# A one-core hybrid attention/mLSTM layer: earlier operand tiles for the second token span, weight sums formed on the fly, and mixer results left in SBUF

## The chip, the cores and the metric

The kernel runs on one core of a Trainium2 chip. The metric is device time in microseconds of one launch; lower is better. The engines are TensorE (PE; its weight loads are shown apart as PEld), VectorE (DVE), ScalarE (ACT), GpSimd (POOL) and SyncE (SP, which here issues nearly all DMAs). SBUF is the memory beside the engines, PSUM holds eight banks that matmuls accumulate into, and DRAM is the chip's far memory.

## What is computed

One layer of an encoder for 2048 tokens of width 1024, in float32. Cut to what matters:

```python
xn = rms_norm(x, mix_norm_g)
aq, ak, av, mq, mk, mv, mo, ipre, fpre, ga, gm = split(xn @ w_in)
att = chunk_band_attention(aq, ak, av, rel_bias)         # 8 heads of 64, own chunk of 64 and 8 before it
mq, mk = silu(causal_conv4([mq, mk]))
hm = mlstm_chunkwise(mq, mk, mv, ipre + b_i, fpre + b_f) # 4 heads of 128, a recurrence over the tokens
m = sigmoid(mo) * headwise_rms_norm(hm)
y = sigmoid(ga) * (att @ w_att_proj) + sigmoid(gm) * (m @ w_mlstm_proj)
x = x + y @ w_out
x = x + square(relu(rms_norm(x) @ w_up)) @ w_down        # hidden width 4096
out = rms_norm(x) * final_norm_g
```

## The kernel before, in words

**Arithmetic.** Every float32 operand is split into a rounded part and a remainder, and each product is three matmuls (high by high, high by low, low by high). The large products also use a seven-product form of 2x2 block multiplication, so each 2x2 block of weights and of operands is turned into seven sums and differences. On the operand side these are called m = 0 to 6, with four tiles (k = 0 to 3) for each m. On the weight side a block is a "quad" of four 512 KB tiles a, b, c, d, and its sums are b-a, d-(b-a), d-b and c-(d-(b-a)).

**Tokens.** The 2048 tokens are four blocks of 512 (b = 0 to 3), in two spans (s = 0: blocks 0 and 1; s = 1: blocks 2 and 3). The stages follow each other on TensorE in `dense` (L832):

1. `token_tiles` (L558): values of blocks 0 and 1.
2. Nine quads of input weights for span 0 (`quad`, L601), in the order `IN_FIRST`. Index i counts them.
3. `in_far` (L665): all input products of span 1, in three batches of operands, `BATCHES = ((0, 3, 1), (2, 4), (5, 6))`, over the eleven weight columns of `IN_ORDER`. Index g counts the batches, i the columns. A partial result goes to a DRAM tensor `park` after batches 0 and 1 (`park_u2`, `park_v`) and comes back through `unpark` (L755), which is started when batch 1 or 2 starts; `finish_far` (L772, its addition is L776) adds it to PSUM. Blocks 0 and 1 of the mixers (attention and mLSTM) run beside it, and `project` (L924) multiplies their results by the two projection weights.
4. Span 0: two quads of `w_out`, eight quads of `w_up`, then `down` (L801), seven times over m, with the mixers of blocks 2 and 3 and their two `project` calls beside it.
5. Span 1: the same two, eight and seven, then the final norm.

**What orders the work.** The program is written by a planner (`Flow`, L104). Each piece of work is a generator that asks for tiles of a pool, waits for events, and then yields the name of an engine, a cost in ns and a delay; the planner grants engines by earliest start, then by priority (0 first), and emits the instructions in that order. So each engine, and SP's DMA queue, runs a fixed order of instructions that follows from estimates such as `yield "sp", 900, 2000` (a 256 KB transfer) and `yield "sp", 1750, 2000` (512 KB). On the chip an instruction that waits holds up everything behind it on its engine or queue.

**Pools.** `wraw` (4 tiles of 512 KB, weights as loaded), `wsp` (3 tiles, split weights), `r` (28 tiles, split operands), `ctx` (16 tiles of 256 KB), `tmp` (6 tiles of 256 KB), `bias` (2), `sc` (4), and the eight PSUM banks.

**Weights.** `loader` (L388) follows `weights` (L357). A quad comes in one of three ways:

- `part`, seven loads: three given tiles and four sums that `sum_w` (L420) formed earlier and stored in the DRAM tensor `wsum`. `sum_w` takes four `ctx` tiles twice, for eight loads, eight subtractions (L437) and eight stores of 256 KB.
- `quad` with `kept` true (`quad_w`, L499): four loads of 512 KB into all four `wraw` tiles, four subtractions of 128x1024 (L512), and four stores of the sums to `wsum` for a later use.
- `quad` with `kept` false: the same without the stores. Before the change nothing uses this.

`SUMS` (L59) lists which quad's sums are formed at which place: seven from the start of the kernel through stage 2 (among them both `w_out` quads and the first two `w_up` quads), two in batch 0 of stage 3, one in batch 1, five in the `w_up` quads of span 0. Every weight tile is then split by ACT (L493) and DVE (L495).

**Operands of span 1.** `stats_far` (L1007) reads blocks 2 and 3 of x, sixteen pieces one after the other through one `tmp` tile at a time, and forms each block's scale (POOL, L1027). `rows_far(1)` spreads the scales over the partitions. `take_x1` (L1607) for each k takes five `tmp` tiles at once, loads four pieces of x (L1615), scales them (L1618), forms the seven sums (L1678) and stores them to the DRAM tensor `xu` (L1957). These are started at i = 5 of stage 2. `take_batches` (L784) reads them back into `r` tiles (L2011) and splits them when the last quad of stage 2 frees its 28 `r` tiles.

**Mixer results.** An attention unit (`weigh`, L1201) or an mLSTM head (`rec_head`, L1492) stores its result to the DRAM tensor `mix` (`keep_mix`, L1239). `load_mix` (L914) starts eight threads that each wait for one result, take an `r` tile, load it and split it (`take_u1`, L2009; ACT L1079, DVE L1084), and `project` waits for all eight.

**Down operands.** `take_u` (L1994) takes 8 `r` tiles (16 in span 1) as a ring for the squared `w_up` results that `down` reads back from the DRAM tensor `u`; it is started at the last but one `w_up` quad. For span 0, `reserve` (L797) then takes 8 more for the results of block 2, and `mixers(2)` starts attention and recurrence, which take `r` tiles as well.

Of the kernel before, what the change touches and what calls it, by code (L numbers as in the profile page):

```python
# [30 lines left out]
D = 1024  # L31
# [218 lines left out]
class Layer:  # L250
# [106 lines left out]
    def weights(self):  # L357
# [62 lines left out]
    def sum_w(self, q, after=()):  # L420
# [3 lines left out]
        for h in range(2):  # L424
# [5 lines left out]
            for n, x in ((0, a), (1, c), (3, d), (2, b)):  # L430
                yield "sp", 900, 2000
# [12 lines left out]
    def load_w(self, src, raw, ev):  # L444
        yield "sp", 1750, 2000
# [3 lines left out]
    def split_w(self, i, src, raw, sent=None):  # L449
# [4 lines left out]
        yield "sp", 1750, 2000  # L454
# [6 lines left out]
    def split_first(self, src, raw, sent):  # L461
# [5 lines left out]
        for k, ev in enumerate(evs):  # L467
            yield "sp", 900, 2000
# [30 lines left out]
    def quad_w(self, i, q, kept, raws, evs):  # L499
# [5 lines left out]
        def keep(n, raw):  # L505
            yield "sp", 1750, 2000
# [158 lines left out]
    def in_far(self, A, aev, ring):  # L665
# [7 lines left out]
        for g, batch in enumerate(BATCHES):  # L673
            got = [[[None, None] for _ in range(2)] for _ in IN_ORDER]
            gev = [[E2() for _ in range(2)] for _ in IN_ORDER]
            room = Pool([0] * (4 + 2 * g))
            if g > 0:
                fl.spawn(self.unpark(g, kept, got, gev, room), 1)
            if g == 1:
                self.load_mix(0, ring)  # L680
            for i, name in enumerate(IN_ORDER):
                self.sum_at(g + 1, i)
                if (g, i) in PROJ_IN:
                    b = PROJ_IN[g, i]
                    yield from self.project(b, ring)
                    if b == 0:
                        fl.spawn(self.take_batch(BATCHES[2], A, aev, ring), 1)
                        self.load_mix(1, ring)
# [66 lines left out]
    def unpark(self, g, kept, got, gev, room):  # L755
        for i, name in enumerate(IN_ORDER):
            o = off(name)
            for x in range(g)[::-1]:
                for n in range(2):
# [4 lines left out]
                    yield "sp", 900, 2000  # L764
# [32 lines left out]
    def reserve(self, room, n, after=()):  # L797
        yield "wait", list(after)
        for _ in range(n):
            self.fl.put(room, *(yield "get", self.rpool, 1))  # L800
    def down(self, s, m, ring, A, aev, blocks, room):  # L801
# [4 lines left out]
        for c in range(4):  # L806
            for b in blocks:
                if PROJ[b][1] == c:
                    yield from self.project(b, room)
                    if b == 2:  # L810
                        self.load_mix(3, room)
# [20 lines left out]
    def dense(self):  # L832
# [15 lines left out]
        for i, name in enumerate(IN_FIRST):  # L848
# [8 lines left out]
            if i == 5:  # L857
# [11 lines left out]
        for s in range(NS):  # L869
# [6 lines left out]
            for i in range(N_F):  # L876
# [37 lines left out]
    def load_mix(self, b, room):  # L914
        for x in range(8):
            self.fl.spawn(self.load_mix1(b, x, room), 1)

    def load_mix1(self, b, x, room):
        B = self.blk[b]
        yield "wait", [B["mix_ev"][x]]  # L920
        (r,) = yield "get", room, 1
        B["mix"][x] = r
        yield from self.take_u1(self.mixd.ap()[b, x], r, B["mixed"][x])
# [19 lines left out]
    def load_gates(self, b, gates, go):  # L943
# [4 lines left out]
        for j in range(0, KT, 2):  # L948
            yield "wait", [go[j // 2]] if j > 0 else self.blk[b]["mix_ev"][:7]
            for x in range(2):  # L950
                for n in range(2):
# [3 lines left out]
                    yield "sp", 900, 2000  # L955
# [51 lines left out]
    def stats_far(self):  # L1007

        fl, nc = self.fl, self.nc
        for b in (2, 3):  # L1010
            r, q = self.rin[b], self.rq
            for t in range(NT):
                for g in range(2):
                    (x,) = yield "get", self.temp, 1
                    x5 = x[:, :T]
                    yield "sp", 900, 2000
# [33 lines left out]
    def square_in(self, b, k, x, tot, ev):  # L1050
# [5 lines left out]
        yield "sp", 900, 2000  # L1056
# [33 lines left out]
    def attention(self, b):  # L1090
# [6 lines left out]
        for j in range(4):  # L1097
# [3 lines left out]
            for x, to in zip((b, b - 1), vs):  # L1101
                yield "sp", 900, 2000
# [4 lines left out]
            for i in range(2):  # L1107
                h = 2 * j + i
                k, q = yield "get", self.rpool, 2
                fl.spawn(self.head(b, h, vs, k, q), 1)  # L1110
        fl.set(B["kq_all"])
        yield "wait", B["head_done"]
        fl.put(self.rpool, *pt)
    def head(self, b, h, vs, k, q):
# [3 lines left out]
        for n, x in ((0, b - 1), (1, b)):  # L1118
# [3 lines left out]
            yield "sp", 900, 2000  # L1122
# [3 lines left out]
        yield "sp", 900, 2000  # L1126
# [74 lines left out]
    def weigh(self, b, h, u, pieces, slots, pev, done):  # L1201
# [30 lines left out]
        fl.put(self.banks, bk)  # L1232
        yield "dve", dve_ns(256)
        nc.vector.tensor_add(tmp[own, :256], tmp[own, :256], tmp[own, 256:512])
        cols = slice(u * 256, u * 256 + 256)
# [3 lines left out]
    def keep_mix(self, b, x, dst, src, pool, *items):  # L1239
        fl, B = self.fl, self.blk[b]  # L1240
        yield "sp", 900, 2000
        self.nc.sync.dma_start(dst, src)
        fl.put(pool, *items)
        B["mix_left"][x] -= 1
        if B["mix_left"][x] == 0:
            fl.set(B["mix_ev"][x])

# [53 lines left out]
    def gates(self, b, bk, less=None, more=False):  # L1301
# [5 lines left out]
        if more:  # L1307
            (add,) = yield "get", self.temp, 1
            yield "wait", [self.gate_ev]
            yield "sp", 900, 2000  # L1310
# [157 lines left out]
    def load_rec(self, b, h):  # L1468
# [5 lines left out]
        for to, x in ((k, MH + h), (q, h)):  # L1474
            yield "wait", [self.m_ev[b, x]]
            yield "sp", 900, 2000
# [3 lines left out]
        yield "sp", 900, 2000  # L1480
# [11 lines left out]
    def rec_head(self, b, h, r):  # L1492
# [75 lines left out]
        yield "sp", 900, 2000  # L1568
# [867 lines left out]
```

## Time and profile before

| | |
|---|---|
| device time, 3 runs | median 2812.18 us (2805.07 to 2813.29) |
| profiled execution, its own time | 2812.02 us |
| its span, first to last instruction | 2810.2 us |
| ACT busy | 1538.8 us (55%) |
| POOL busy | 37.6 us (1%) |
| weight loads, PEld busy | 2280.1 us (81%) |
| moved by DMA | 737.50 MB, mean 262 GB/s |
| weight tiles loaded as given, from `wf` | 188 of 512 KB |
| sums loaded from `wsum` | 176 of 512 KB |
| DVE, splits of weights (L495) | 453 x 1220 ns |
| DVE, subtractions of 128x1024 (L512) | 56 x 1219 ns |
| DVE, subtractions of 128x512 in `sum_w` (L437) | 120 x 684 ns |

How to read it: a view by windows gives, for each stretch of the span, the busy time of every engine, the granted clock of TensorE as a mean share of full speed, and the share of time that the sixteen DMA engines moved packets. A matmul is recorded from its start until its result is out, so consecutive matmuls overlap; when TensorE never waits, starts follow each other closely and its busy time equals the stretch. "idle before <- X" is time in which an engine stood still and what ended it.

### The profile page before, as it was taken

Reading aid. Unit: us, or ns where it says so; the run is one execution under the profiler, and the core shown is the slowest. Engines: PE = TensorE matmul, PEld = TensorE weight load, DVE = VectorE, ACT = ScalarE, POOL = GpSimd, SP = SyncE. Lnnn points to the kernel's source line nnn. Section 1 sums busy time; section 2 is a strip of 40 time slices with the busy share of each in tenths; the row PEclk is TensorE's granted clock in tenths of the full one; section 3 lists DMA queues with packets and bytes.
Section 4 is the critical chain, followed back from the end, with each engine's and each line's share of the span. In section 5 each row is a group of like instructions: output and inputs, shape, how many; then the busy total and the mean of one; then the engine's idle time right before and its main releaser. Section 6 shows DMA issues by size and latency. Waiting matters only on the chain.

```text
span 2810.2 us, 38516 instructions
## 1 busy us (share of the span) xinstructions
PE 2752.5 (98%) x12916; PEld 2280.1 (81%) x12916; DVE 2053.5 (73%) x3684; ACT 1538.8 (55%) x2636; POOL 37.6 (1%) x108
## 2 busy tenths in 40 slices
PE   9999997999999999999999999999999999999998
PEld 8778886788888777788888887888888888888887
DVE  7877765887887767885777789778877664457675
ACT  6545454765663433565555676566444665555443
POOL 0000000000000000000000000000000000000000
PEclk9999998999999999999999999999999999999999
DMA  8777689888888899977878887877777475578773
GB/s 283 274 257 258 238 288 301 277 273 272 265 297 290 300 311 321 318 247 266 309 270 292 272 277 239 249 217 244 258 266 245 169 260 206 205 268 271 268 250 128
DMA packets 353402, 737.50 MB, mean 262 GB/s; under 512 B 39524, under 2 KB 66788, under 8 KB 353204
## 3 DMA queue, kind: packets, MB, share of 16 engines
q1 hardware_dynamic: 353060, 735.04, 77.7%
q8 instruction: 101, 1.65, 0.2%
q14 instruction: 97, 0.79, 0.1%
q10 hardware_dynamic: 144, 0.01, 0.0%
HBM read 498.89 MB, written 236.01 MB: 262 GB/s over the span
## 4 chain that ended last, share of the span: by engine, by line
PE 80%; DVE 7%; DMA 6%; issue 3%; ACT 2%; SPq 1%; POOL 0%; POOLq 0%; ACTq 0%; DVEq 0%
PE bank L623 38%; PE bank L554 8%; PE bank L555 8%; PE bank L556 8%; PE bank L654 8%; PE bank L1218 2%; PE bank L1291 2%; DVE wsp L495 2%; PE bank L659 2%; PE bank L1260 2%; DMA ctx<-park 1%; DMA r<-u 1%; DMA r<-mix 1%; ACT wsp L493 1%; DVE sc L1266 1%
## 5 line engine op out<-in xcount | busy, mean ns | idle before, releaser
L623 PE MATMUL bank<-r,wsp 128*128 128x512 f32 x4872 | 1114.5, 390 | 2.7 <-ACT r L1081 1.0
L623 PEld LDWEIGHTS bank<-r,wsp 128*128 128x128 f32 x4872 | 912.8, 188 | 198.3 <-issue 1.9
L493 ACT CAST wsp<-wraw 128x1024 fp32r<-128x1024 f32 x453 | 475.9, 1051 | 525.0 <-PE bank L623 221.2
L495 DVE TENSOR_TENSOR wsp<-wraw,wsp 128x1024 fp32r<-128x1024 f32 x453 | 552.7, 1220 | 287.3 <-ACT wsp L493 275.8
L554 PE MATMUL bank<-r,wsp 128*128 128x512 f32 x1152 | 454.8, 395 | 2.3 <-ACT r L1079 1.7
L555 PE MATMUL bank<-r,wsp 128*128 128x512 f32 x1152 | 449.5, 390 | 0.0
L556 PE MATMUL bank<-r,wsp 128*128 128x512 f32 x1152 | 448.9, 390 | 0.0
L654 PE MATMUL bank<-r,wsp 128*128 128x512 f32 x1512 | 373.3, 395 | 5.3 <-DVE ctx L776 4.6
L654 PEld LDWEIGHTS bank<-r,wsp 128*128 128x128 f32 x1512 | 278.8, 189 | 62.9 <-DVE ctx L776 3.5
L556 PEld LDWEIGHTS bank<-r,wsp 128*128 128x128 f32 x1152 | 216.3, 188 | 45.8
L554 PEld LDWEIGHTS bank<-r,wsp 128*128 128x128 f32 x1152 | 216.4, 188 | 44.4 <-ACT r L1079 2.1
L555 PEld LDWEIGHTS bank<-r,wsp 128*128 128x128 f32 x1152 | 216.6, 188 | 40.6 <-DVE r L1084 0.2
L1079 ACT CAST r<-r 128x512 fp32r<-128x512 f32 x284 | 171.7, 621 | 121.2 <-DMA r<-u 89.9
L1084 DVE TENSOR_TENSOR r<-r 128x512 fp32r<-128x512 f32 x284 | 188.8, 685 | 65.0 <-ACT r L1079 64.2
L1711 DVE TENSOR_TENSOR ctx<-bank,ctx 128x512 f32<-128x512 f32 x150 | 103.1, 688 | 96.5 <-PE bank L623 96.0
L1272 ACT ACTIVATE sc<-sc,scs 128x640 f32<-128x640 f32 (+4 forms) x128 | 97.3, 760 | 65.5 <-DVE scs L1266 64.9
L1703 ACT COPY ctx<-bank 128x512 f32<-128x512 f32 x150 | 87.0, 581 | 56.9 <-PE bank L623 55.9
L2027 ACT ACTIVATE ctx<-ctx 128x512 f32<-128x512 f32 x96 | 60.5, 630 | 84.0 <-DVE ctx L1711 83.9
L1296 DVE TENSOR_TENSOR r<-bank,r 128x512 fp32r<-128x512 f32 (+1 forms) x168 | 95.8, 592 | 11.7 <-ACT r L1294 11.1
L1218 PE MATMUL bank<-r,r 128*128 128x512 f32 x336 | 97.9, 373 | 4.5 <-DVE r L1296 3.1
L1260 PE MATMUL bank<-r,r 128*128 128x320 f32 (+3 forms) x480 | 91.2, 309 | 5.9 <-DMA r<-kfar 2.6
L1294 ACT CAST r<-bank 128x512 fp32r<-128x512 f32 (+1 forms) x168 | 80.5, 517 | 22.6 <-PE bank L1291 20.0
(246 smaller groups left out, 2996.3 us busy)
## 6 DMA issues: line engine op xcount, KB each, us to landing
wraw<-in_wf SPq DMA_DIRECT2D x188, 512.0 KB, 4.5
wraw<-wsum SPq DMA_DIRECT2D x176, 512.0 KB, 4.4
r<-u SPq DMA_DIRECT2D x224, 256.0 KB, 4.5
u<-ctx SPq DMA_DIRECT2D x128, 256.0 KB, 2.3
ctx<-in_wf SPq DMA_DIRECT2D x120, 256.0 KB, 4.3
wsum<-ctx SPq DMA_DIRECT2D x120, 256.0 KB, 3.8
wsum<-wraw SPq DMA_DIRECT2D x56, 512.0 KB, 3.3
u<-tmp SPq DMA_DIRECT2D x96, 256.0 KB, 3.0
```

Source lines behind the costliest of these rows:

```text
L493: nc.scalar.copy(w[:, 0], raw)
L495: nc.vector.tensor_sub(w[:, 1], raw, w[:, 0].bitcast(F32))
L554: mm(ps, lh, rh, start=first, stop=False)
L555: mm(ps, lh, rl, start=False, stop=False)
L556: mm(ps, ll, rh, start=False, stop=last)
L623: mm(ps, wv[:, x, k, n], a[:, y], start=new and k == 0 and x == y == 0, stop=k == 3 and x == 1, skip_group_check=True)
L654: mm(ps, wv[:, x, k, n], a[:, y], start=start and x == y == 0, stop=stop and x == 1, skip_group_check=True)
L1079: self.nc.scalar.copy(dst[:, 0], src)
L1084: self.nc.vector.tensor_sub(dst[:, 1], src, dst[:, 0].bitcast(F32))
L1218: nc.tensor.matmul(bkv[:, :, c0:c0 + w], st, sl[:, :, o:o + w], start=n == 0, stop=n == total - 1)
L1260: nc.tensor.matmul(bks[x][:, :w], q[:, y, i * P:(i + 1) * P], kf[:, f * P + x * w:f * P + x * w + w], start=y == 0, stop=y == 1)
L1711: nc.vector.tensor_add(t[:, o:o + 512], ps, t[:, o:o + 512])
```

## The change

- **Operands early.** `rows_far(1)` and the four `take_x1` start at i = 2 of stage 2 and no longer at i = 5.
- **Weights on the fly.** All `w_out` and `w_up` quads, in both spans, come as `quad` with `kept` false. `SUMS` drops the four quads that were summed ahead for them; the eight `w_down` quads are summed at two places in batch 0 of stage 3 and six in the `w_up` quads of span 0.
- **Mixer results on chip.** `take_mix` takes the eight `r` tiles of a block at once, where `load_mix` was started. A result of block 2, and of any other block once those tiles are there, is split straight into them by ACT and DVE; only other results go through `mix`.
- **Order of tiles at the end of `w_up`, span 0.** `take_u` and `reserve` wait until the first two attention heads of block 2 have their tiles (`begun`), and `take_u` is started one quad later.
- **Park early.** `unpark` for batch 2 starts at the last column of batch 1, with the same room of eight tiles.
- **Planner.** The cost of a 256 KB transfer on SP is 800 instead of 900, of a 512 KB one 1570 instead of 1750, everywhere; the seven operands of a k get priorities by m.

The diff's core (the SP costs, repeated on many lines, are shown once):

```diff
+DIRECT = (2,)
 N_IN = 16
-N_USUM = 2
-SUMS = {(0, n): q for n, q in enumerate((Q_IN[IN_FIRST[0]], Q_VM, Q_VM + 1, N_G, N_G + 1, N_G + N_O, N_G + N_O + 1))}
-SUMS.update({at: N_Q - N_F + n for n, at in enumerate(((1, 2), (1, 7), (2, 2), (4, 0), (4, 1), (4, 2), (4, 3), (4, 4)))})
+SUMS = {(0, n): q for n, q in enumerate((Q_IN[IN_FIRST[0]], Q_VM, Q_VM + 1))}
+SUMS.update({at: N_Q - N_F + n for n, at in enumerate(((1, 4), (1, 8), *((4, i) for i in range(6))))})
...
-            yield from (part(q, m) for q in range(N_G, N_G + N_O) for m in range(7))
-            for q in range(N_G + N_O, N_G + N_O + N_F):
-                if s == 0 and q >= N_G + N_O + N_USUM:
-                    yield "quad", (q, True)
-                else:
-                    yield from (part(q, m) for m in range(7))
+            for q in range(N_G, N_G + N_O + N_F):
+                yield "quad", (q, False)
...
-        yield "sp", 1750, 2000
+        yield "sp", 1570, 2000
...
-            if g == 1:
-                self.load_mix(0, ring)
+            if g == 1:
+                fl.spawn(self.take_mix(0, ring), 1)
             for i, name in enumerate(IN_ORDER):
                 self.sum_at(g + 1, i)
+                if g == 1 and i == len(IN_ORDER) - 1:
+                    ahead = ([[[None, None] for _ in range(2)] for _ in IN_ORDER], [[E2() for _ in range(2)] for _ in IN_ORDER],
+                             Pool([0] * 8))
+                    fl.spawn(self.unpark(2, kept, *ahead), 1)
...
-            if i == 5:
+            if i == 2:
                 ready, read = Event(), [Event() for _ in range(4)]
                 fl.spawn(self.rows_far(1, ready, read), 2)
                 for k in range(4):
                     fl.spawn(self.take_x1(k, ready, read[k]), 2)
...
-                    fl.spawn(self.take_u(s, ring, *D), 0)
+                    if s == 1:
+                        fl.spawn(self.take_u(s, ring, *D), 0)
                 if s == 0 and i == N_F - 1:
-                    fl.spawn(self.reserve(room, 8, self.blk[2]["vp_ev"][:1]), 0)
-                    self.load_mix(2, room)
+                    fl.spawn(self.take_u(s, ring, *D, self.blk[2]["begun"]), 0)
+                    fl.spawn(self.reserve(room, 8, self.blk[2]["begun"]), 0)
+                    fl.spawn(self.take_mix(2, room), 1)
                     self.mixers(2)
...
+        direct = self.direct(b, h // 2)
         yield "dve", dve_ns(256)
         nc.vector.tensor_add(tmp[own, :256], tmp[own, :256], tmp[own, 256:512])
-        cols = slice(u * 256, u * 256 + 256)
+        if direct:
+            yield "wait", [B["mix_got"]]
+            r = B["mix"][h // 2]
+            yield "act", act_ns(256)
+            nc.scalar.copy(r[own, 0, cols], tmp[own, :256])
+            yield "dve", dve_ns(256)
+            nc.vector.tensor_sub(r[own, 1, cols], tmp[own, :256], r[own, 0, cols].bitcast(F32))
+            fl.put(self.temp, tmp)
+            self.mix_done(b, h // 2)
+            fl.set(done)
+            return
...
+    def direct(self, b, x):
+        how, got = self.blk[b]["how"], self.blk[b]["mix_got"]
+        return how.setdefault(x, b in DIRECT or got.at is not None)
...
+    def take_mix(self, b, room):
+        B = self.blk[b]
+        B["mix"] = yield "get", room, 8
+        self.fl.set(B["mix_got"])
...
-        fl.spawn(self.keep_mix(b, 4 + h, self.mixd.ap()[b, 4 + h], kt[:, :512], self.ctx, kt), 1)
+        if self.direct(b, 4 + h):
+            yield "wait", [B["mix_got"]]
+            yield from self.split(kt[:, :512], B["mix"][4 + h])
+            self.mix_done(b, 4 + h)
+            fl.put(self.ctx, kt)
+        else:
+            fl.spawn(self.keep_mix(b, 4 + h, self.mixd.ap()[b, 4 + h], kt[:, :512], self.ctx, kt), 1)
...
-            fl.spawn(give(m, dst), 1)
+            fl.spawn(give(m, dst), 1 + m / 100)
```

More of the change, by code (lines that the diff above doesn't have):

```diff
@@ L673, in in_far @@
         for g, batch in enumerate(BATCHES):
[L674 to L677, printed above, removed]
+            if g < 2:
+                got = [[[None, None] for _ in range(2)] for _ in IN_ORDER]
+                gev = [[E2() for _ in range(2)] for _ in IN_ORDER]
+                room = Pool([0] * (4 + 2 * g))
+            else:
+                got, gev, room = ahead
+            if g == 1:
                 fl.spawn(self.unpark(g, kept, got, gev, room), 1)
             if g == 1:
-                self.load_mix(0, ring)
+                fl.spawn(self.take_mix(0, ring), 1)
             for i, name in enumerate(IN_ORDER):
                 self.sum_at(g + 1, i)
+                if g == 1 and i == len(IN_ORDER) - 1:
+                    ahead = ([[[None, None] for _ in range(2)] for _ in IN_ORDER], [[E2() for _ in range(2)] for _ in IN_ORDER],
+                             Pool([0] * 8))
+                    fl.spawn(self.unpark(2, kept, *ahead), 1)
                 if (g, i) in PROJ_IN:
@@ L687, in in_far @@
                         fl.spawn(self.take_batch(BATCHES[2], A, aev, ring), 1)
-                        self.load_mix(1, ring)
+                        fl.spawn(self.take_mix(1, ring), 1)
                     else:
@@ L795, in take_batch, with reserve @@
                 fl.spawn(self.take_u1(self.xud.ap()[m, k], r, aev[m][k]), 0)
-    def reserve(self, room, n, after=()):
-        yield "wait", list(after)
+    def reserve(self, room, n, after=None):
+        if after is not None:
+            yield "wait", [after]
         for _ in range(n):
@@ L810, in down @@
                     if b == 2:
-                        self.load_mix(3, room)
+                        fl.spawn(self.take_mix(3, room), 1)
                     else:
@@ L912, in mixers @@
             fl.spawn(self.attention(b), 1)
[L914 to L923, printed above, removed]
     def project(self, b, room):
@@ L1110, in attention @@
                 fl.spawn(self.head(b, h, vs, k, q), 1)
+            if j == 0:
+                fl.set(B["begun"])
         fl.set(B["kq_all"])
@@ L1246, in keep_mix, with load_mix @@
             fl.set(B["mix_ev"][x])
+            if self.direct(b, x):
+                fl.set(B["mixed"][x])
+            else:
+                fl.spawn(self.load_mix(b, x), 1)
+    def direct(self, b, x):
+        how, got = self.blk[b]["how"], self.blk[b]["mix_got"]
+        return how.setdefault(x, b in DIRECT or got.at is not None)
+    def load_mix(self, b, x):
+        B = self.blk[b]
+        yield "wait", [B["mix_got"]]
+        yield from self.take_u1(self.mixd.ap()[b, x], B["mix"][x], B["mixed"][x])
+    def take_mix(self, b, room):
+        B = self.blk[b]
+        B["mix"] = yield "get", room, 8
+        self.fl.set(B["mix_got"])
     def scores(self, b, i, k, q, bias, sct, ev):
@@ L1626, in load @@
             yield "wait", [kept[b][j]]
-            yield queue, 900, 2000
+            yield queue, 800, 2000
             self.nc.sync.dma_start(a, src[b].ap()[j])
@@ L1955, in store @@
     def store(self, dst, src, ev, pool=None, item=None, queue="sp"):
-        yield queue, 900, 2000
+        yield queue, 800, 2000
         self.nc.sync.dma_start(dst, src)
@@ L1991, in square_kept, with take_u @@
         self.fl.set(summed[j])
-    def take_u(self, s, ring, A, aev):
+    def take_u(self, s, ring, A, aev, after=None):
         fl = self.fl
+        if after is not None:
+            yield "wait", [after]
         for _ in range(N_RING[s]):
```

58 lines of the change are left out of this document (32 added, 26 removed).

## The prediction

> **What bounds the kernel now.** I read the page first (busy times, then the shares of the chain that ended last), then the chain in order of time, then the windows by stage.
>
> ```profile
> PE 2752.5 (98%) x12916; PEld 2280.1 (81%) x12916; DVE 2053.5 (73%) x3684; ACT 1538.8 (55%) x2636; POOL 37.6 (1%) x108
> ...
> PE 80%; DVE 7%; DMA 6%; issue 3%; ACT 2%; SPq 1%; POOL 0%; POOLq 0%; ACTq 0%; DVEq 0%
> ```
>
> ```profile
> 1175.50 202.99 PE bank L623 x894
> ```
>
> TensorE bounds it. A busy share of 98% alone would not say so, since recorded matmuls overlap; the chain does: 894 matmuls in 202.99 us, one every 227 ns, with nothing between them. The change touches no matmul, so their number times 227 ns stays, and all it can win is time in which TensorE stands still or runs slowly. The windows say where that is (columns: length, busy time and instructions of PE, PEld, DVE, ACT, POOL, granted clock, DMA share, GB/s):
>
> ```profile
> 125.00:460.00 335.00, 335.00 (x1501) 275.12 (x1500) 246.62 (x374) 168.93 (x263) 2.22 (x4) 1.00 0.75 264
> 460.00:510.00 50.00, 32.63 (x150) 25.78 (x150) 31.04 (x89) 24.91 (x74) 2.70 (x7) 0.73 0.94 299
> 510.00:715.00 205.00, 202.66 (x1095) 170.59 (x1094) 162.63 (x444) 132.27 (x300) 7.23 (x26) 1.00 0.85 271
> 715.00:960.00 245.00, 244.03 (x1204) 204.76 (x1203) 201.24 (x407) 132.20 (x234) 3.59 (x13) 1.00 0.86 286
> 960.00:1030.00 70.00, 62.02 (x272) 48.64 (x270) 46.52 (x67) 31.54 (x43) 0.00 (x0) 0.98 0.92 315
> 1030.00:1180.00 150.00, 144.61 (x616) 115.96 (x617) 119.48 (x176) 66.02 (x94) 0.00 (x0) 0.99 0.93 316
> 1180.00:1540.00 360.00, 360.00 (x1590) 296.96 (x1589) 253.74 (x361) 208.67 (x313) 0.69 (x5) 1.00 0.79 278
> 1540.00:1700.00 160.00, 156.57 (x847) 132.61 (x846) 129.13 (x312) 105.02 (x232) 6.17 (x17) 1.00 0.87 272
> 1700.00:1790.00 90.00, 82.75 (x435) 68.42 (x435) 74.05 (x207) 56.67 (x119) 2.39 (x11) 0.98 0.78 234
> 1790.00:2102.00 312.00, 310.80 (x1558) 262.50 (x1557) 255.14 (x520) 172.39 (x319) 4.77 (x15) 1.00 0.77 249
> 2102.00:2485.00 383.00, 383.00 (x1687) 316.37 (x1686) 229.06 (x298) 221.86 (x331) 0.00 (x0) 1.00 0.64 222
> ```
>
> The quads of stage 2 (125 to 460) and the output and up quads (1180 to 1540, 2102 to 2485) lose nothing. The losses are A, the start of `in_far` (460 to 510: 17.4 us idle, clock 0.73); B, the start of its third batch (960 to 1030: 8.0 us idle); and C, the mixers beside `down` (1540 to 1790: 3.4 and 7.3 us idle). Each is worked out below.
>
> **Term A, operands early.** The scalings of x for span 1 (one row per k), the stores of the sums, the forming of the scales, and one and the same piece of work (eight matmuls of L1523) before and inside the loss:
>
> ```profile
> L1618 DVE SCALAR_TENSOR_TENSOR tmp<-tmp,gcol,bias x4: 741/742/743, 307.8 to 325.2; 128x512 f32<-128x512 f32 x4
> L1618 DVE SCALAR_TENSOR_TENSOR tmp<-tmp,gcol,bias x4: 741/743/744, 375.0 to 381.3; 128x512 f32<-128x512 f32 x4
> L1618 DVE SCALAR_TENSOR_TENSOR tmp<-tmp,gcol,bias x4: 744/746/747, 423.3 to 439.0; 128x512 f32<-128x512 f32 x4
> L1618 DVE SCALAR_TENSOR_TENSOR tmp<-tmp,gcol,bias x4: 743/748/752, 479.9 to 486.4; 128x512 f32<-128x512 f32 x4
> ```
>
> ```profile
> L1957 SPq DMA_DIRECT2D xu<-tmp x28: 319/427/1056, 310.2 to 508.1; - x28
> ```
>
> ```profile
> L1027 POOL TENSOR_TENSOR r_in<-r_in,half x2: 1006/1006/1007, 210.1 to 275.5; 128x4 f32<-128x4 f32 x2
> ```
>
> ```profile
> 456.20 1.05 PE L1523 MATMUL bank<-r 128*128 128x128 f32 x8
> ...
> 480.55 2.07 PE L1523 MATMUL bank<-r 128*128 128x128 f32 x8 [0.24 <-DMA r<-mfar]
> ```
>
> `in_far` begins at 460, its first product needs m = 0 of all four k, and the last k is only scaled from 479.9 on. So TensorE has nothing but scraps of the mixers, and after the standstill it runs at half speed (2.07 us for what took 1.05). The loss lies between the idle time, 50 - 32.6 = 17.4 us, and that plus all clock missing, (1 - 0.73) x 50 = 13.5 us: 30.9 us. I call it about 28.
>
> A quad is 168 matmuls, 38.1 us. Starting three quads earlier is 114 us, but not all of that counts: the scales of block 3 are there only at 275.5 + 1.0 us. Then come the spreading over the partitions and the first scaling; so k = 0 can be scaled from about 280, 28 us earlier. The four k follow each other 57 us apart ((479.9 - 307.8) / 3). If that pitch stays, the last k starts at 452, its sums go out and come back some 15 us later, and most of the loss is gone. I expect a shorter pitch, since what slows it is shared and gets lighter: dropping four `sum_w` takes 64 transfers of 256 KB out of stage 2, 16.8 MB of 335 us x 264 GB/s = 88 MB. The reads of x (2 x 8 pieces) and the 28 stores are only moved within a stage whose DMA share is 0.75. **A: -26 us**, leaving 2 us as in the windows behind it; ends -17 (idle alone, half of the rest left) and -31.
>
> **Weights on the fly.**
>
> ```profile
> L1084 DVE TENSOR_TENSOR r<-r 128x512 fp32r<-128x512 f32 x284 | 188.8, 685 | 65.0 <-ACT r L1079 64.2
> L1079 ACT CAST r<-r 128x512 fp32r<-128x512 f32 x284 | 171.7, 621 | 121.2 <-DMA r<-u 89.9 <-DMA r<-mix 24.1 <-DMA r<-xu 3.3
> ...
> L437 DVE TENSOR_TENSOR ctx<-ctx,ctx 128x512 f32<-128x512 f32 x120 | 82.0, 684 | 9.2 <-DMA wsum<-ctx 5.8 <-DMA ctx<-in_wf 2.5
> ...
> L512 DVE TENSOR_TENSOR wraw<-wraw,wraw 128x1024 f32<-128x1024 f32 x56 | 67.8, 1219 | 1.7 <-DMA wsum<-wraw 1.3
> ...
> L1234 DVE TENSOR_TENSOR tmp<-tmp 64x256 f32<-64x256 f32 x64 | 26.7, 417 | 1.2
> ```
>
> Removed: 4 x 8 subtractions x 0.684 = 21.9 us of DVE, and with them 64 transfers of 256 KB; 24 stores of 512 KB (the six `kept` quads); 14 x 3 loads of 512 KB (four instead of seven). That is 16.8 + 12.6 + 22.0 = 51 MB. Added: 14 x 4 subtractions x 1.219 = 68.3 us of DVE: 19.5 in span 0, 48.8 in span 1. In span 1 DVE goes from 229.1 to 277.9 of 383 us, 73%; TensorE hides it, as it already hides a DVE of 70% in 1180 to 1540, where six quads of this kind ran (24 of the 56 subtractions) and PE was busy 360.00 of 360.00 us. Without that cover each quad would cost its four subtractions, 4.9 us. The one place with little cover is the first output quad, at the end of 1030 to 1180: DVE 80% busy, PE already losing 5.4 us. There I take **+2 us**, between 0 and 4.9.
>
> **Term B, park early.**
>
> ```profile
> PE bank L659 <- DVE ctx L776: 5.2, 1, 5.2
> PE bank L654 <- DVE ctx L776: 4.6, 5, 1.4
> ```
>
> ```profile
> L765 SPq DMA_DIRECT2D ctx<-park x18: 423/444/1067, 972.5 to 1026.3; - x18
> ```
>
> TensorE waits for the addition L776, which waits for parked tiles, the first of which is issued at 972.5, in the middle of the loss. Idle 8.0 plus 0.02 x 70 of clock is 9.4 us; the two waits sum to 9.8. Eight tiles asked for one column earlier (48 matmuls, 11 us) cover the first two columns; one `sum_w` (4.2 MB of this stretch's 70 us x 315 GB/s = 22 MB) leaves as well. **B: -7 us**, between -2 (only the first short waits go) and -9.
>
> **Term C, mixer results on chip.**
>
> ```profile
> 1728.69 2.21 DMA mix<-tmp
> 1730.97 4.34 DMA r<-mix
> ...
> 1772.01 5.27 DMA r<-mix
> ```
>
> The chain of waits runs through the trip to DRAM just before `project(2)`: 2.2 and 4.3 us, and once more 5.3. A result kept on chip has no such trip. The split remains: for an mLSTM head the same ACT and DVE instruction; for attention 16 half-height pairs instead of four full ones, DVE 16 x 0.417 - 4 x 0.685 = +3.9 us a block, ACT 16 of at most 0.621 (no row has this form) less 4 x 0.621, at most +7.5; both spread over 200 us beside TensorE. New is a wait: the first heads of block 2 hold `tmp`, `bias` and `r` tiles until `take_mix(2)` has its eight, which the last up quad frees within 38 us. Also, block 2's heads now get their tiles before `down`'s ring. C's idle time is 3.4 + 7.3 us, 1.8 with the clock on top, 12.5 together. **C: -7 us**, the last trip and the loose end before it; between 0 (the recurrence sets the end, not the trips) and -12.
>
> Against it: `down`'s ring gets its eight tiles after ten for the mixers. The last quad frees four per step of 5.44 us, so the 18th comes after step five, at 27 of 38 us; load 4.3 to 5.3, split 0.6 + 0.7: ready with some 4 us to spare if SP's queue is free. **+2 us**, between 0 and 8.
>
> The moved sums of the down weights and the changed planner costs issue what was issued before, in another order, under stages that lose nothing: 0.
>
> **Sum.** -26 - 7 - 7 + 2 + 2 = -36 us. The profiled execution took 2812.0 us by itself (span 2810.2, 1.8 around it), 0.2 from the median of the runs. So **2776 us**. All good ends: -31 - 9 - 12 = -52, 2760. All poor ends: -17 - 2 - 0 + 4.9 + 8 = -6, 2806.
>
> **A rule to weigh.** The Trainium skill, page "DMA: Bandwidth & Descriptors", section "Queues, rings and completion order", says that each DMA engine consumes the descriptors of one queue in the order of its ring. By it, eight tiles asked for early stand ahead of weights issued after them. No row of before shows a weight tile held up so. The third rival is what it would do here.
>
> **The rivals.**
>
> 1. *A shrinks only in part.* The k keep their pitch or lose some, since each needs five of six `tmp` tiles at once and the key quad's pieces (L1821) want them too. For it: the pitch was 48 to 67 us. Against: the traffic around it is lighter. A -12, C -4, the rest as above: 2793.
> 2. *Slower: `tmp` held too early.* k = 0 now takes five of the six `tmp` tiles at about 205 and keeps them until the scales are there; but the sixteen loads for these scales need a `tmp` tile too, at the lowest priority, and the last query pieces another. Block 3's eight loads took 275.5 - 210.1 = 65.4 us with free choice of tiles. It decides at 304: scales later than that put k = 0 later than now. If the eight take twice as long in the one tile left, the scales come at 341, k = 0 at 345, the last k at 345 + 172 = 517, 37 us later than now, and TensorE stands still for as long: +37 for A, -7 - 7 + 4 for the rest: 2839. Against it: the loads went through one tile after the other before as well, and the stage moves 17 MB less.
> 3. *B is not late but full.* With DMA at 0.92 to 0.93, 2.1 MB of parked tiles asked for early take 2.1 MB / 315 GB/s = 6.7 us from the weights behind them, and B is given back: -29, 2783.
> 4. *The change does less than it says.* If the results of blocks 0, 1 and 3 are all finished before their tiles are there, they go through DRAM as before, and C falls away: -29, also 2783.
>
> **How the numbers follow.** Forecast 0.60 (own range 2760 to 2795); rival 1 0.15; rival 2 0.11; rivals 3 and 4 together 0.14. About 0.3%, 8.4 us, can be told from no change. Rival 2 is the slower case; of rival 1 and of the poorest ends together 0.04 fall within 8.4 us; the rest is faster, 0.85. The range goes from all good ends to all poor ones, 2759 to 2806, and leaves out rival 2.
>
> **What would show it.** Right: the last store to `xu` before 455, and PE busy at full clock where `in_far` starts; 112 subtractions at L512's place and 88 at L437's, with the quads of span 1 still without idle time; no wait for parked tiles at the third batch; no load from `mix` ahead of `project(2)`. Wrong: idle time in stage 2, waits for weight splits in the output and up quads, or a gap where `down` starts. The forecast fails if the planner's new order opens waits in stretches that lose nothing now; no row can exclude that.

## The result and the profile after

The changed kernel takes 2767.3 us (median of 4 runs, 2766.6 to 2769.7), against 2812.7 us before: 45.4 us less, a ratio of 0.9838 with a 95% interval of 0.9807 to 0.9869. The profiled execution took 2766.6 us, its span 2764.9.

The page after, its busy times and the shares of the chain that ended last:

```profile
PE 2733.3 (99%) x12916; PEld 2268.9 (82%) x12916; DVE 2098.3 (76%) x3719; ACT 1552.8 (56%) x2667; POOL 42.2 (2%) x108
...
PE 82%; DVE 8%; DMA 3%; issue 3%; ACT 3%; POOL 1%; SPq 0%; POOLq 0%; ACTq 0%; DVEq 0%
```

TensorE still runs 12916 matmuls. Its idle time fell from 2810.2 - 2752.5 = 57.7 to 2764.9 - 2733.3 = 31.6 us, and the same matmuls were busy 19.2 us less, as the mean granted clock rose from 0.992 to 0.999. The two together are the whole gain.

Where it came from, by windows of the changed kernel (columns as in the prediction). The third batch now starts 21 us earlier, so 939 to 1009 answers to 960 to 1030 of before, and 1009 to 1150 to the stretch behind it; 1503 to 2056 is `down` of span 0 with the mixers:

```profile
125.00:460.00 335.00, 333.20 (x1489) 271.84 (x1488) 243.87 (x371) 171.06 (x266) 6.19 (x8) 1.00 0.72 252
460.00:510.00 50.00, 48.41 (x276) 40.99 (x275) 34.17 (x109) 32.53 (x85) 2.82 (x8) 1.00 0.87 261
939.00:1009.00 70.00, 69.25 (x307) 55.56 (x307) 50.68 (x74) 35.39 (x51) 0.00 (x0) 1.00 0.92 316
1009.00:1150.00 141.00, 140.31 (x618) 115.28 (x617) 117.79 (x170) 63.62 (x89) 0.00 (x0) 1.00 0.89 305
...
1503.00:2056.00 553.00, 548.08 (x2842) 463.15 (x2841) 466.61 (x1056) 351.40 (x706) 13.15 (x43) 1.00 0.76 239
2058.00:2440.00 382.00, 381.27 (x1678) 314.62 (x1677) 266.21 (x329) 216.89 (x325) 0.00 (x0) 1.00 0.52 182
```

The stage that answers to 1503 to 2056, in the kernel before:

```profile
1538.00:2102.00 564.00, 552.12 (x2848) 465.19 (x2846) 460.32 (x1039) 336.05 (x672) 13.33 (x43) 1.00 0.80 253
```

Loss A: idle 17.4 became 1.6 us and the clock 0.73 became 1.00. Loss B: 8.0 became 0.8. Loss C: 564 - 552.1 = 11.9 became 553 - 548.1 = 4.9. The quads of span 1 (2058 to 2440) idle 0.7 us with DVE at 266 of 382 us.

The operands of span 1 after, their scalings and their stores, and the forming of the scales:

```profile
L1656 DVE SCALAR_TENSOR_TENSOR tmp<-tmp,gcol,bias x16: 740/744/750, 245.7 to 386.0; 128x512 f32<-128x512 f32 x16
```

```profile
L1995 SPq DMA_DIRECT2D xu<-tmp x28: 319/402/782, 252.9 to 399.9; - x28
```

```profile
L1023 POOL TENSOR_TENSOR r_in<-r_in,half x2: 1006/2694/4382, 197.0 to 249.7; 128x4 f32<-128x4 f32 x2
```

All sums are on their way by 400, 108 us earlier than before. That fits the prediction's picture of A. The experiments show that the time does not come from it.

### The profile page after: what moved, and what is told of

The parts are those of the page before. It is cut to its first block, busy times and chain, and to the rows that moved or that the text cites. A ratio compares the mean times of both kernels' runs of the same rounds, so it can differ in the third digit from the quotient of the medians.

```text
span 2764.9 us, 38314 instructions
## 1 busy us (share of the span) xinstructions
PE 2733.3 (99%) x12916; PEld 2268.9 (82%) x12916; DVE 2098.3 (76%) x3719; ACT 1552.8 (56%) x2667; POOL 42.2 (2%) x108
## 4 chain that ended last, share of the span: by engine, by line
PE 82%; DVE 8%; DMA 3%; issue 3%; ACT 3%; POOL 1%; SPq 0%; POOLq 0%; ACTq 0%; DVEq 0%
PE bank L619 35%; PE bank L551 9%; PE bank L550 9%; PE bank L552 9%; PE bank L650 9%; PE bank L655 2%; PE bank L1216 2%; PE bank L1323 2%; DVE wsp L491 2%; PE bank L1292 2%; DVE r L1080 1%; DMA ctx<-in_xt 1%; DVE sc L1298 1%; ACT wsp L489 1%; PE bank L1378 1%
## 5 line engine op out<-in xcount | busy, mean ns | idle before, releaser
L1080 DVE TENSOR_TENSOR r<-r 128x512 fp32r<-128x512 f32 x271 | 180.3, 686 | 52.5 <-ACT r L1075 51.0
L1075 ACT CAST r<-r 128x512 fp32r<-128x512 f32 x271 | 163.3, 622 | 92.1 <-DMA r<-u 72.6
L508 DVE TENSOR_TENSOR wraw<-wraw,wraw 128x1024 f32<-128x1024 f32 x112 | 136.2, 1218 | 2.5 <-DMA wsum<-wraw 1.4
```

The source lines that it names most:

```text
L508: V.tensor_sub(dst, x, y)
L1075: self.nc.scalar.copy(dst[:, 0], src)
L1080: self.nc.vector.tensor_sub(dst[:, 1], src, dst[:, 0].bitcast(F32))
```

## The experiments

Each run was compared with runs of the kernel before on the same chip; "lost beside down" and the like is a stage's length less PE's busy time in it.

| run | median us (range) | ratio to before, 95% interval |
|---|---|---|
| changed kernel | 2767.3 (2766.6 to 2769.7) | 0.9838 (0.9807 to 0.9869) |
| x1_late | 2767.1 (2765.6 to 2769.9) | 0.9850 (0.9836 to 0.9865) |
| sums_ahead | 2794.1 (2792.0 to 2798.3) | 0.9947 (0.9932 to 0.9962) |
| mix_far | 2774.2 (2773.3 to 2777.1) | 0.9873 (0.9857 to 0.9890) |
| park_late | 2770.5 (2769.9 to 2771.8) | 0.9862 (0.9847 to 0.9877) |
| x1_only | 2815.0 (2809.5 to 2818.2) | 1.0006 (0.9997 to 1.0015) |
| fly_only | 2775.4 (2769.5 to 2777.9) | 0.9862 (0.9845 to 0.9879) |
| costs_only | 2777.9 (2775.5 to 2780.2) | 0.9874 (0.9859 to 0.9889) |
| late_ahead | 2788.0 (2784.2 to 2789.4) | 0.9908 (0.9893 to 0.9923) |
| fly_costs | 2773.8 (2769.6 to 2776.9) | 0.9858 (0.9841 to 0.9876) |
| old_costs | 2782.7 (2781.7 to 2783.4) | 0.9892 (0.9875 to 0.9908) |
| costs_low | 2773.6 (2770.3 to 2775.0) | 0.9857 (0.9842 to 0.9872) |
| ring_first | 2772.5 (2767.2 to 2774.0) | 0.9851 (0.9835 to 0.9868) |

The theory after the result was the prediction's: A went because the operands start earlier, B because parked tiles are asked for earlier, C because results stay on chip. Its rival: something common to all, SP's queue as the planner sees it.

### x1_late: the early start undone

```diff
-            if i == 2:
+            if i == 5:
                 ready, read = Event(), [Event() for _ in range(4)]
```

> The changed kernel with one thing undone: the operands of span 1 are started at i = 5 again. Theory 1 (the early start is what removed the loss at the start of in_far): scalings start near 305 as before the change, the last stores to xu come after 460, TensorE stands still there for 17 us or more, and the time is 2767 + 20 to 28 = 2787 to 2795 us. Theory 2 (the lighter SP queue did it: fewer weight sums and smaller planner costs shorten the pitch from 57 to the 44 us that the changed kernel shows): last k at 305 + 3 x 44 = 437, stores done by about 455, no loss, 2767 to 2773 us.

No loss shows: 2767.1 us. Its window at the start of `in_far`, and its stores:

```profile
459.00:510.00 51.00, 47.88 (x250) 39.67 (x248) 34.70 (x102) 34.01 (x82) 1.71 (x6) 0.93 0.83 265
```

```profile
L1995 SPq DMA_DIRECT2D xu<-tmp x28: 319/383/692, 308.1 to 486.7; - x28
```

The scalings start at 307 as before the change, and A is gone all the same but for a rest (3.1 us idle, clock 0.93). Even the last store at 487, later than theory 2 had it, does no harm: only the first batch's operands are needed at 460. Theory 2 holds in the time: the changed kernel does not need the early start.

### sums_ahead: weights as before

```diff
+N_USUM = 2
-SUMS = {(0, n): q for n, q in enumerate((Q_IN[IN_FIRST[0]], Q_VM, Q_VM + 1))}
+SUMS = {(0, n): q for n, q in enumerate((Q_IN[IN_FIRST[0]], Q_VM, Q_VM + 1, N_G, N_G + 1, N_G + N_O, N_G + N_O + 1))}
...
-                yield "quad", (q, False)
+                if s == 0 and q >= N_G + N_O + N_USUM:
+                    yield "quad", (q, True)
+                else:
+                    yield from (part(q, m) for m in range(7))
```

(The places of the down sums in `SUMS` are put back as well, and the `w_out` quads are parts again.)

> The changed kernel with the output and up weights as before: four quads summed ahead, six up quads stored in span 0 and loaded in span 1. Theory 1 (weights on the fly cost TensorE nothing and won nothing by themselves): 2765 to 2770 us, with DVE some 46 us less busy and some 51 MB more moved. Theory 2 (the bytes they save are what shortened the other waits): pitch of the four k back near 57 us, waits for parked tiles again, 2775 to 2790 us.

27 us slower than the changed kernel, far beyond what the weights on the fly were expected to matter. But the loss is not at A: the operands still start at i = 2. It is in the second batch of `in_far` and beside `down`:

```profile
753.00:969.00 216.00, 201.75 (x936) 167.57 (x935) 158.88 (x296) 96.15 (x163) 2.84 (x8) 0.97 0.87 292
1528.00:2089.00 561.00, 551.34 (x2842) 462.33 (x2841) 471.43 (x1063) 345.45 (x695) 12.74 (x42) 1.00 0.73 233
```

14.2 us idle in a batch that loses 195 - 193.0 = 2.0 us in the changed kernel, and 9.7 instead of 4.9 beside `down`. In that batch TensorE waits most for two steps of DVE: 6.6 us for the split of the attention's weights (L1334), 5.3 us for additions to parked results (L760). Theory 2 was nearer, but the time is 4 us above its range and the places are not those that it named. The edit also moves the sums of the down weights back, one of them into this very batch; which of its parts costs the time was not tested.

### mix_far: results through DRAM again

```diff
-        return how.setdefault(x, b in DIRECT or got.at is not None)
+        return how.setdefault(x, False)
```

> The changed kernel with every mixer result sent through DRAM again (the eight r tiles are still taken at once). Theory 1 (the trip to DRAM ahead of project(2) was the end of term C): TensorE waits for loads from mix again beside down, 5 to 10 us, 2772 to 2778 us. Theory 2 (term C went because the heads of block 2 get their tiles first and SP's queue is lighter): 2765 to 2769 us.

7 us slower than x1_late, which ran beside it on the same chip and differs by the early start as well. That is theory 1's time, and the loss is in the stage that it named, the one beside `down`:

```profile
1504.00:2066.00 562.00, 551.19 (x2843) 463.27 (x2842) 460.76 (x1039) 344.95 (x687) 12.95 (x43) 1.00 0.77 247
```

10.8 us idle instead of 4.9, the stage 9 us longer. The wait, though, is not the one that theory 1 named. Who waits for loads from `mix` in this stage is ACT, which splits them:

```profile
  ACT r L1075: 12.1, 11
```

In the changed kernel ACT does not wait for them there. TensorE itself waits only 0.4 us for such a split (L1080), and longer for steps of the mixers on ACT and DVE, the longest of them first:

```profile
PE bank L1323 <- ACT sc L1311: 2.7, 3, 1.3
...
PE bank L551 <- DVE r L1080: 0.4, 1, 0.4
```

So results on chip are worth about 7 us. That the loads hold up ACT, and ACT the mixers, fits, but was not shown.

### park_late: parked tiles asked for late again

```diff
-            if g < 2:
+            if True:
...
-            else:
-                got, gev, room = ahead
-            if g == 1:
+            if g > 0:
                 fl.spawn(self.unpark(g, kept, got, gev, room), 1)
...
-                if g == 1 and i == len(IN_ORDER) - 1:
+                if g == 1 and i == len(IN_ORDER):
```

> The changed kernel with the parked tiles of the third batch asked for only when that batch starts. Theory 1 (term B was late asking): idle time of 3 to 8 us returns in the first 70 us of the third batch, 2770 to 2776 us. Theory 2 (term B was a full DMA queue, relieved by the weight sum that left this stretch): 2765 to 2769 us.

3.4 us slower than x1_late beside it (their runs touch at 2769.9), at the foot of theory 1's range. But at the place that theory 1 named, the first 70 us of the third batch, little of it returns, 1.6 us idle against 0.8:

```profile
945.00:1015.00 70.00, 68.37 (x302) 54.50 (x301) 51.86 (x77) 34.86 (x50) 0.00 (x0) 1.00 0.90 306
```

So asking early is worth about 3 us at most, and hardly at B; the rest of loss B went for another reason.

### x1_only, fly_only, costs_only: one part alone on the kernel before

x1_only is the reverse of x1_late's edit on the kernel before. fly_only takes the changed kernel's `SUMS` and `quad` lines. costs_only is:

```diff
-        yield "sp", 900, 2000
+        yield "sp", 800, 2000
...
-        yield "sp", 1750, 2000
+        yield "sp", 1570, 2000
```

> The kernel before with one thing changed: the operands of span 1 start at i = 2. In the changed kernel the early start could be undone without loss (2767.1 us), so either the early start and the lighter queue can each do it alone, or only the lighter queue can. Theory 1 (each alone): scalings from about 250 to 280, last store to xu before 455, the loss at the start of in_far gone, 2812 - 25 = 2784 to 2790 us. Theory 2 (only the lighter queue): the last store to xu still comes after 460 and the time is 2800 to 2815 us.

> The kernel before with only the weights changed: output and up quads summed on the fly, the sums of the down weights at the new places, operands still started at i = 5, old planner costs. Theory 1 (the four dropped weight sums free stage 2 and the moved one frees the third batch): pitch of the four k near 40 us, losses A and B both shrink, 2812 - 30 = 2778 to 2788 us. Theory 2 (the planner's lower costs of a transfer are needed for it): 2800 to 2815 us.

> The kernel before with only the planner's costs of a transfer lowered (800 and 1570). Theory 1 (costs alone let the low priorities through): pitch of the four k well under 57 us and A smaller by 10 us or more, 2785 to 2802 us. Theory 2 (they only reorder): 2805 to 2820 us.

x1_only gains nothing, ratio 1.0006, though loss A is gone. Two windows of it, A's place and the start of the output quads:

```profile
460.00:510.00 50.00, 47.67 (x269) 39.44 (x268) 42.41 (x127) 38.37 (x101) 2.00 (x8) 1.00 0.90 276
...
1131.00:1180.00 49.00, 34.31 (x116) 24.07 (x115) 38.68 (x58) 20.68 (x31) 0.00 (x0) 0.86 0.79 276
```

The 15 us of idle time avoided at 460 are given back: 14.7 us idle at 1131, with the clock down to 0.86. There TensorE waits for the operands of the first output quad. Their loads in the kernel before and in x1_only, and, for x1_only from 1120 to 1180, the splits of these operands on ACT (L1081), what ACT waited for and who waited for the splits:

```profile
L1628 SPq DMA_DIRECT2D ctx<-yp x32: 319/425/692, 1076.2 to 2100.7; - x32
```

```profile
L1628 SPq DMA_DIRECT2D ctx<-yp x32: 319/428/1223, 1118.8 to 2103.3; - x32
```

```profile
L1081 ACT ACTIVATE r<-ctx x24: 612/630/635, 1124.9 to 1173.9; 128x512 fp32r<-128x512 f32 x24
...
  DMA ctx<-yp: 12.7, 5
...
  PE bank L623: 12.5, 4
```

The first matmul of the output quads starts 16 us earlier (1128.0, before 1144.1), but these loads begin 43 us later. Neither theory had this: A went, as theory 1 said, and the time stayed, as theory 2 said.

fly_only and costs_only each gain most of the 45 us, 37 and 34, with the operands still started at i = 5. Both went the way of their theory 1, and beyond its range (2778 to 2788 and 2785 to 2802). costs_only moves the same 737.5 MB: it is an edit of estimates, which takes no work away. Its windows at A and at the start of the output quads:

```profile
460.00:510.00 50.00, 49.72 (x265) 41.32 (x264) 32.12 (x79) 30.66 (x75) 1.99 (x8) 1.00 0.94 307
...
1122.00:1170.00 48.00, 46.31 (x204) 37.79 (x203) 35.89 (x51) 21.17 (x30) 0.00 (x0) 1.00 0.94 316
```

### late_ahead: early start and weights both undone

sums_ahead with x1_late's edit.

> The changed kernel with both undone: operands at i = 5 and the weights summed ahead as before. Summing ahead alone made 2794.1 us, with no loss at the start of in_far. Theory 1 (early start and dropped sums stand in for each other): A comes back, 15 to 30 us on top, 2809 to 2824 us. Theory 2 (the lower costs alone keep the queue light enough): last store to xu before 460 and 2792 to 2797 us.

2788.0 us, 6 us faster than sums_ahead and outside theory 1's range. With the lower costs A does not come back: 4.6 us are idle from 460 to 510, though operands are stored up to 486, not before 460 as theory 2 had it. What it loses against x1_late lies, as in sums_ahead, in the second batch (7.1 us idle from 762 to 960) and beside `down` (9.2 us). Theory 2 was nearest, 4 us off.

### fly_costs, old_costs, costs_low, ring_first

fly_costs is fly_only with costs_only's edit. old_costs is the changed kernel with the reverse of that edit, costs_low the changed kernel with 700 and 1370. ring_first:

```diff
-                    if s == 1:
-                        fl.spawn(self.take_u(s, ring, *D), 0)
+                    fl.spawn(self.take_u(s, ring, *D), 0)
                 if s == 0 and i == N_F - 1:
-                    fl.spawn(self.take_u(s, ring, *D, self.blk[2]["begun"]), 0)
```

> The kernel before with the weights on the fly and the planner's lower costs of a transfer, nothing else. Alone they made 2775.4 and 2777.9 us. Theory 1 (both do one thing: they let the planner's full SP queue issue the waiting transfers earlier, so together they give little more): 2768 to 2776 us, losses A and B gone, C as in the two alone (16 to 20 us of lost time beside down). Theory 2 (two separate gains): 2750 to 2762 us.

> The changed kernel with the planner's old costs of a transfer (900 and 1750). Theory 1 (the lighter queue from the weights on the fly is enough): 2766 to 2773 us. Theory 2 (with the early start of the operands it is not, as the early start alone gave its gain back where the output quads begin): waits for operands of the first output quad come back, 2778 to 2792 us.

> The changed kernel with still lower planner costs of a transfer: 700 for 256 KB and 1370 for 512 KB, that is 375 and 383 GB/s, more than any slice of these traces moved (321). Theory 1 (the costs only have to be no higher than the chip's): 2764 to 2769 us. Theory 2 (the plan must match the chip, an estimate too low opens waits for transfers): 2772 to 2785 us.

> The changed kernel with the ring of the down operands asked for at the last but one up quad again, ahead of the mixers' tiles. Theory 1 (the heads of block 2 going first is part of term C): 3 to 8 us more lost beside down, 2770 to 2775 us, and no gap where down starts. Theory 2 (only the trip through DRAM counted, and the ring going second costs about 2 us): 2764 to 2768 us.

fly_costs: 2773.8 us, theory 1. The two do not add up: 37 and 34 alone, 40 together. What is left to the changed kernel, 6.5 us, is the size that mix_far measured for the results on chip, though the intervals of fly_costs and of the changed kernel overlap. The stage beside `down` fits: it idles 11.3 us here, where results go through DRAM.

```profile
1505.00:2067.00 562.00, 550.73 (x2848) 463.83 (x2847) 461.49 (x1042) 338.48 (x675) 14.58 (x43) 1.00 0.79 248
```

old_costs: 2782.7 us, theory 2 in size, slower than fly_only, which has the same costs and none of the other parts (their intervals just overlap). But the output quads do not wait; the loss is beside `down`, 12.7 us idle against 4.9:

```profile
1506.00:2072.00 566.00, 553.29 (x2842) 465.68 (x2842) 474.86 (x1073) 346.14 (x702) 12.98 (x43) 0.99 0.76 238
```

Results on chip and the old costs together win nothing there; why the order comes out so was not settled.

costs_low: 2773.6 us, in theory 2's range and 6 us above the changed kernel's median, but the intervals overlap: no gain, and whether there is a loss stays open. ring_first: 2772.5 us, in theory 1's range, but the intervals overlap (0.9835 to 0.9868 against 0.9807 to 0.9869), and the loss beside `down` that theory 1 named is not there, 4.0 us against 4.9: inconclusive.

```profile
1505.00:2060.00 555.00, 550.96 (x2849) 463.07 (x2848) 469.81 (x1063) 343.45 (x695) 14.71 (x43) 1.00 0.76 237
```

No version beat the changed kernel beyond the noise.

## Why the prediction was right in the time and wrong in a cause

**What bounds the kernel.** Right. The gain is idle time and slow clock of TensorE in the three places named, and no stretch that lost nothing before loses more than 2 us now (stage 2, 125 to 460, loses 1.8).

**Term A, -26 us.** The size was about right (the third batch starts 21 us earlier), the cause wrong. The step that failed is "operands early": an early start alone (x1_only) clears A and gives it back at the output quads, and without it (x1_late) A is gone too. What clears it there is the pitch, 57 us before, and still 52 in x1_only. In x1_late, the sixteen scalings and the last group of four:

```profile
L1656 DVE SCALAR_TENSOR_TENSOR tmp<-tmp,gcol,bias x16: 741/746/752, 307.1 to 432.9; 128x512 f32<-128x512 f32 x16
```

```profile
L1656 DVE SCALAR_TENSOR_TENSOR tmp<-tmp,gcol,bias x4: 742/744/746, 415.8 to 432.9; 128x512 f32<-128x512 f32 x4
```

That is (415.8 - 307.1) / 3 = 36 us. On the kernel before, lower costs alone or weights on the fly alone do much the same; the sixteen scalings of costs_only and of fly_only (in the kernel before the last starts at 486):

```profile
L1618 DVE SCALAR_TENSOR_TENSOR tmp<-tmp,gcol,bias x16: 743/746/755, 307.4 to 431.5; 128x512 f32<-128x512 f32 x16
```

```profile
L1614 DVE SCALAR_TENSOR_TENSOR tmp<-tmp,gcol,bias x16: 743/748/755, 306.8 to 438.0; 128x512 f32<-128x512 f32 x16
```

The prediction named the dropped weight sums as a help to the pitch; with them, or with the lower costs, no early start was needed. That the gain could be given back at the end of `in_far`, whose DMA share of 0.93 stood in its own rows, was missing from the sum.

**Weights on the fly, counted +2 us.** The counts were right: 112 and 88 subtractions, DVE up, 0.7 us idle in the quads of span 1. The +2 us at the first output quad did not come: 1009 to 1150 idles 0.7 us.

```profile
L508 DVE TENSOR_TENSOR wraw<-wraw,wraw 128x1024 f32<-128x1024 f32 x112 | 136.2, 1218 | 2.5 <-DMA wsum<-wraw 1.4
...
L433 DVE TENSOR_TENSOR ctx<-ctx,ctx 128x512 f32<-128x512 f32 x88 | 60.1, 683 | 10.4 <-DMA wsum<-ctx 10.2
```

Its worth was missed: alone it gains 37 us, and undone it loses 27 (both with the places of the down sums).

**Planner costs, counted 0.** Wrong: alone they gain 34 us. "Issued in another order, under stages that lose nothing" overlooked that the order also decides who is late in the stages that do lose. A reading that fits is argued and not shown: 262144 bytes in 900 ns are 291 GB/s, and over `in_far` the kernel before moved just that, while costs_only moved more:

```profile
460.00:1150.00 690.00, 658.32 (x3214) 544.49 (x3214) 535.55 (x1143) 370.89 (x720) 13.51 (x46) 0.98 0.88 291
```

```profile
458.00:1122.00 664.00, 651.16 (x3226) 540.71 (x3225) 524.61 (x1122) 371.80 (x726) 14.32 (x47) 0.99 0.88 297
```

By this reading SP was full in the plan, so transfers of low priority (the operands of span 1 among them) were put off, while the chip still moved 315 GB/s in the kernel before from 960 to 1030. Fewer bytes (fly_only moved 281 GB/s over `in_far`) or a lower estimate would then both take SP off the plan's critical path and stand in for each other. No run shows the plan itself, and x1_only moved 294 GB/s at the old costs. costs_low found nothing more to gain below these costs.

**Term B, -7 us.** Size right in its window (8.0 to 0.8 us idle), cause mostly not: the early request is worth 3 us at most by park_late, and costs_only, without it, idles only 2.3 us there (951 to 1022). The stretch behind it gained too, from 5.4 us idle (1030 to 1180) to 0.7 (1009 to 1150); the sum had nothing for that.

**Term C, -7 us.** Right in size (mix_far: 7 us, idle time 11.9 to 4.9). The cause is right only in part: results on chip are needed for it, but with them the stage still idles 12.7 us at the old costs (old_costs) and 9.7 with the weights as before (sums_ahead), and the trip itself was not TensorE's wait in mix_far. The reserve of +2 us for the ring was not needed: 1470 to 1560, where `down` starts, idles 0.5 us.

**The sum, -36 us.** It came out 9 us short, and the parts are off more than the whole. The third batch starts at 946 instead of 967, `down` of span 0 at 1503 instead of 1538, the quads of span 1 at 2057 instead of 2102. So 21 us were gained up to the third batch (26 in the sum), 14 from there to `down` (7 - 2 = 5) and 10 in `down` (5). These shares are rough, since mixer work runs beside each stage. That the total came so near is in part luck. The low end of the range, 2759, is 1 us below its own sum of good ends.

**The rivals.** The first did not come: the pitch went from 57 us to (376.9 - 245.7) / 3 = 44. Nor did the second: the last scales are formed at 249.7 instead of 275.5, so `tmp` held early did no harm. The third, parked tiles that hold up weights, did not show: without the early request the kernel was slower. The Trainium skill, page "DMA: Bandwidth & Descriptors", section "Queues, rings and completion order", whose rule stood beside it, is neither borne out nor contradicted: no view here shows a weight tile behind a parked one. The fourth came true in part. Of 32 results, 19 still come through `mix`, 16 of them before `down`, that is all of blocks 0 and 1:

```profile
L2051 SPq DMA_DIRECT2D r<-mix x19: 319/320/1480, 745.9 to 1808.0; - x19
```

C did not need those, since its loss lies beside `down`.

## What to carry to other kernels

A loss that an edit removes may have been removed by another part of the same change: undo each part alone, and do each part alone, before a cause is named. Where a planner writes the order, try its estimate of a shared queue by itself: here it cost 34 us. Compare the rate that it allows with the rate that the trace moves. A wait taken away ahead of a stage whose DMAs are nearly full can be given back at that stage's end, as in x1_only.

## What the runs showed of the hardware that was not expected

Of two equal power operations on 128x4 elements on POOL in the changed kernel (L1023) one took 1.01 us and the other 4.38, and TensorE waited 1.8 us for it. The 4.38 us stand in mix_far, sums_ahead, park_late and ring_first too; both took 1.01 us in the kernel before. The cause was not looked into, and spans on POOL are rough. In x1_only the DMA engines moved 331 GB/s over 111 us, above any slice of the pages of before (321) and of costs_only (328):

```profile
1020.00:1131.00 111.00, 106.68 (x460) 86.98 (x459) 78.64 (x112) 43.08 (x57) 0.00 (x0) 0.98 0.94 331
```
